# A hybrid attention layer on one core: masked score sums and their maximum in one VectorE operation, and rotary operands laid out for two heads at a time

## The chip, the cores and the metric

The kernel runs on one core of one Trainium2 chip. The metric is the device time in microseconds (us) of one execution. Before the change it is 898.43 us, the median of three runs (897.34 to 899.4). TensorE (PE) multiplies matrices into PSUM, VectorE (DVE) and ScalarE (ACT) do the element work, GpSimd (POOL) issues some of the transfers, and SyncE (SP) issues the rest.

## The reference, cut to what matters

One decoder layer, 512 tokens, width 2048, all in float32. The normed input is projected once and split; eight MLA heads and eight forgetting (FoX) heads run side by side, each output is gated, and one output projection and a norm follow.

```python
h = _rms_norm(x, g_pre); proj = h @ w_in                    # 2048 -> latents, gates, fq, fk, fv, f_logit
# FoX head: c is the running sum of the log forget gates
c = cumsum(log_sigmoid(f_logit + b_forget))
logits = (q @ k.T) * HEAD_DIM**-0.5 + c[q_pos] - c[k_pos]
# MLA head: 128 plain columns, 64 rotary columns; the rotary key is shared by all heads
logits = (q_nope @ k_nope.T + rope(q_rope) @ rope(k_rope).T) * QK**-0.5
# both: causal mask, softmax over keys, in blocks of 128 queries
p = softmax(where(key <= query, logits, -inf)); o = p @ v
out = x + _rms_norm(concat(o_mla * silu(gate_mla), o_fox * silu(gate_fox)) @ w_out, g_post)
```

The term c[q_pos] is the same for a whole row of logits, and a softmax over the row does not depend on it.

## The kernel before, in words

**Products.** Every large product is made of three passes (`mm3`, L149 to L151): each operand is split into a high part and a low part, rounded by ScalarE (`act.copy`) and subtracted by VectorE, and high times high, high times low and low times high are summed in PSUM. Weight chunks of 512 KB come in on SP's queue (`load`), ScalarE writes `whi` (L276), VectorE writes `wlo` (L279). Several projections are done with seven block products in place of eight, which gives VectorE additional block sums (L266, L946).

**Order of the work.** The program is straight-line code. Small work (scores, transposes of probabilities, values, splits) is put into a list `todo`, and `pump` takes entries from it between the matmuls of a projection; `drain` empties it. A planner then orders each engine's instructions by its own costs and the program's priorities; a few instructions are pinned with `in_order`. Big tiles (4 KB per partition) come from a pool of 28 slots.

**Stages.** 0 to 40 us: first columns of the input projection. 40 to 235 us: FoX gates, values, first queries and keys. 235 to 435 us: four FoX pairs of heads; the scores of one pair are pumped into the next pair's projections. 435 to 600 us: latents and MLA gates. 600 to 750 us: four MLA pairs. From 718 us on: output projection.

**A block of scores** (`Head.scores`, from L616) serves one head and 128 queries `b`; it holds n = 128(b+1) keys in one PSUM bank of the three of `att_bank`. For b = 0 the operands are whole float32 blocks; for the others two or three passes per kind of column. Then, before the change:

- FoX: `ccol` holds c per query. VectorE adds c[q] - c[k] in place in PSUM, once for the columns below the diagonal block (L636) and once for the diagonal block, whose key row has the mask added (L639). MLA: the mask is added to the diagonal block in place (L630).
- VectorE takes the negated row maximum (L643); for MLA ScalarE scales it by the query's norm (L649, `qcol`).
- ScalarE takes the exponential from PSUM into the tile `p` in SBUF and sums the row (L650); VectorE divides by the sum (L651, L652).

`forget_cols` (L784) turns c by four transposes on PE into `ccol`. `load_keys` (L790) broadcasts one head's c to 128 partitions by one transfer of 256 KB; `forget_keys` (L795) negates it and adds the mask to its four diagonal blocks.

**Rotary operands.** `rotary_key` (L1103) turns the shared key, 64 rows, and leaves in `kr` its high part in rows 0 to 63 and its low part in rows 64 to 127. It is the last step of the rotary tables (list `rot`, L1193) and runs at 164 to 171 us. Per MLA pair, `rotate` makes two products `a` and `b` of the two heads' 128 rotary rows; four additions of 64 rows (L1514) write each head's turned query twice into a tile `rq`; `rq` is split (L138, L139) for the blocks from 128 on, and its first 128 columns are copied (L126). Both passes multiply by the same `kr`.

Of the kernel before, what the change touches and what calls it, by code (L numbers as in the profile page):

```python
# [43 lines left out]
L4 = KVR // 2  # L44
KL = L4 + ROPE
NSLOT = 28
DEEP, EXTRA = 6, 3
# [18 lines left out]
def tile_hybrid_layer(  # L66
# [42 lines left out]
    def att_bank(name):  # L109
        return bank("at", name, 3)  # L110
# [60 lines left out]
    gains = cst.tile([NK, P], F32, name="gains")  # L171
    gains2 = cst.tile([P, P], F32, name="gains2")
    pool.memset(gains2, 0.0)
    xk = [None] * NK
# [20 lines left out]
    make_identity(nc, ident)  # L195
    mask = cst.tile([P, P], F32, name="mask")
    make_causal_mask(nc, mask, mask_val=NEG)
# [410 lines left out]
    class Head:  # L608
# [7 lines left out]
        def scores(self, b):  # L616
            n = (b + 1) * P
            nn = n
            s = att_bank(f"s{self.name}{b}")
            qs = slice(b * P, n)  # L620
            pairs = []
            if b == 0:
                pairs, nn = self.whole, P
            else:
                for kind, (qh, ql), (kh, kl) in zip(("nope", "rope"), self.q, self.k):
                    pairs += [(qh, kh), (qh, kl), (ql, kh)] if kind == "nope" else [(qh, kh), (ql, kh)]
            for i, (a, c) in enumerate(pairs):
                pe.matmul(s[:, :nn], a[:, qs], c[:, :nn], start=(i == 0), stop=(i == len(pairs) - 1))  # L628
            if self.fox is None:
                dve.tensor_tensor(out=s[:, qs], in0=s[:, qs], in1=mask, op=ALU.add)  # L630
            else:
                nk, nkm, h = self.fox
                cq = ccol[:, b, h : h + 1]
                if b:
                    m = b * P
                    dve.scalar_tensor_tensor(  # L636
                        out=s[:, :m], in0=s[:, :m], scalar=cq, in1=nk[:, :m], op0=ALU.add, op1=ALU.add
                    )
                dve.scalar_tensor_tensor(  # L639
                    out=s[:, qs], in0=s[:, qs], scalar=cq, in1=nkm[:, qs], op0=ALU.add, op1=ALU.add  # L640
                )
            st = pp.tile([P, 3], F32, tag="st", name=f"st{self.name}{b}", bufs=4)
            dve.tensor_reduce(out=st[:, 0:1], in_=s[:, :n], op=ALU.max, axis=AX.X, negate=True)  # L643
            p = pp.tile([P, n], F32, tag=f"p{b}", name=f"p{self.name}{b}")
            unit = 1.0
            if self.fox is None:

                unit = qcol[:, b : b + 1]
                act.mul(st[:, 0:1], st[:, 0:1], unit)  # L649
            act.activation(p, s[:, :n], AF.Exp, bias=st[:, 0:1], scale=unit, accum_out=st[:, 1:2])  # L650
# [61 lines left out]
    pool.memset(rf, 0.0)  # L712
    ccol = cst.tile([P, NT, NH], F32, name="ccol")
    c_dram = dr.tile([NH, S], F32, name="c_dram")
# [17 lines left out]
    def forget_sums(r):  # L732
# [28 lines left out]
        def scan():  # L761
# [17 lines left out]
            two(ln, ln, d, ALU.add),  # L779
            both(z, z, 0.0, ln, ALU.min, ALU.subtract),  # L780
            scan,
        ]

    def forget_cols():  # L784
        pt = att_bank("ccol")
        for t in range(NT):
            pe.transpose(pt[:, t * P : (t + 1) * P], rf[:, t * P : (t + 1) * P], ident)
        dve.tensor_copy(ccol, pt.rearrange("p (t c) -> p t c", t=NT)[:, :, R])

    def load_keys(h):  # L790
        both = slot(f"nk{h}")
        nc.sync.dma_start(both[:, 0, :], c_dram[h : h + 1, :].to_broadcast([P, S]))
        return both, h

    def forget_keys(both, h):  # L795

        nk, nkm = both[:, 0, :], both[:, 1, :]
        in_order(dve.tensor_scalar(out=nk, in0=nk, scalar1=-1.0, scalar2=None, op0=ALU.mult))
        for b in range(NT):
            c = slice(b * P, (b + 1) * P)  # L800
            dve.tensor_tensor(out=nkm[:, c], in0=nk[:, c], in1=mask, op=ALU.add)
        return nk, nkm, h

# [72 lines left out]

    HALF = S // 2
    oper = {}
# [224 lines left out]
    def rotary_key():  # L1103

        a, b = rotate(rf, ROPE, 1.0, "k")
        dve.tensor_tensor(out=a[:ROPE, :], in0=a[:ROPE, :], in1=b[:ROPE, :], op=ALU.add)
        act.copy(kr[:ROPE, :], a[:ROPE, :])
        dve.tensor_tensor(out=kr[ROPE:, :], in0=a[:ROPE, :], in1=kr[:ROPE, :].bitcast(F32), op=ALU.subtract)

    kr = tb.tile([P, S], F32R, name="kr")  # L1110

# [80 lines left out]
    rot = rotary_tables()  # L1192
    rot.append(rotary_key)  # L1193
    wait(1)
# [33 lines left out]
    k = fox_k(0, wholes)  # L1228
    forget_cols()
    drain()  # L1230
# [17 lines left out]
    v_out(c21, 1, 0)  # L1248
    keys = [load_keys(6 + i) for i in range(2)]
    seconds.clear()  # L1250
# [6 lines left out]
    for p in range(4):  # L1257
        if p:
            q, wholes = fox_q(p)
            drain()  # L1260
            keys = [load_keys(2 * (3 - p) + i) for i in range(2)]
            vt = load_v(3 - p, v_slot(3 - p))
# [9 lines left out]
        if p == 2:  # L1272
            nc.sync.dma_start(gains2[0:6, :], g_q.rearrange("o (k p) -> (o k) p", p=P))
            nc.sync.dma_start(gains2[6:10, :], g_kv.rearrange("o (k p) -> (o k) p", p=P))
            make_gcol(gains2, NK, 10)
        vs = values_of(f"fv{3 - p}")
# [41 lines left out]
    lat_diag = {}  # L1318
    qcol = cst.tile([P, NT], F32, name="qcol")

    def latent_stats(j):
# [15 lines left out]
        if j == 0:  # L1337
            dve.scalar_tensor_tensor(out=qcol, in0=y, scalar=SC_M, in1=rcol, op0=ALU.mult, op1=ALU.mult)
            return
# [161 lines left out]
    for p in range(4):  # L1501
# [6 lines left out]
        qw = [[whole_block(wholes, i, qb[i])] for i in range(2)]  # L1508
        a, b = rotate(qb[2], P, 1.0, f"q{p}")
        for i in range(2):  # L1510
            r = tmp(f"rq{p}{i}")
            src = slice(ROPE * i, ROPE * (i + 1))
            for half in range(2):
                dve.tensor_tensor(  # L1514
                    out=r[ROPE * half : ROPE * (half + 1), :], in0=a[src, :], in1=b[src, :], op=ALU.add
                )
# [16 lines left out]
        for i in c["kv"]:  # L1533
            hi, lo = chunk(i)
            for j in range(chunks[i][3]):
# [13 lines left out]
                paced(hi)  # L1549
        k = [[split(kb[i], f"mk{p}{i}"), (kr, None)] for i in range(2)]  # L1550
        kw = [[whole_block(wholes, 2 + i, kb[i]), kr.bitcast(F32)[:, :P]] for i in range(2)]
        drain()
# [238 lines left out]
```

## Time and profile before

| what | value |
|---|---|
| median of three runs | 898.43 us (897.34 to 899.4) |
| the profiled execution | 897.76 us, its span 896.0 us, 1.76 us around it |
| granted TensorE clock, mean | 0.997 |
| PE busy | 883.9 us (99%) |
| VectorE busy | 678.7 us (76%) |
| ScalarE busy | 453.8 us (51%) |
| DMA | 218.26 MB, mean 244 GB/s |

The profile is of one execution. A busy share is the time in which an engine has at least one instruction in flight; matmuls overlap, so the mean duration of a matmul is longer than the distance from one to the next. An "idle before" belongs to the engine just ahead of an instruction, and the name behind it is what ended it.

### The profile page before, as it was taken

What the parts mean: (1) busy time and instruction counts of PE and PEld (TensorE: products, weight loads), DVE (VectorE), ACT (ScalarE), POOL (GpSimd) and SP (SyncE); (2) the same over time, 40 slices, a digit from 0 to 9 for tenths busy, and PEclk for the clock granted to TensorE, in tenths of its full rate; (3) what the DMA queues carried; (4) which work ended last, traced back from release to release, by engine and by line L of the source; (5) the groups of instructions that cost most, each with busy time, mean ns of one, the idle gap of its engine ahead of it and who ended that gap; (6) DMA issues with size and microseconds to landing.
All of it is one profiled execution on the core that took longest, in us unless ns stands there. A gap on an engine that the chain in (4) does not pass through costs nothing.

```text
span 896.0 us, 12851 instructions
## 1 busy us (share of the span) xinstructions
PE 883.9 (99%) x4598; PEld 755.2 (84%) x4598; DVE 678.7 (76%) x1123; ACT 453.8 (51%) x837; POOL 65.7 (7%) x86
## 2 busy tenths in 40 slices
PE   9999999999999999999999999999999999999996
PEld 8988887888888888888998998788888888888885
DVE  4579995648766838577588898967877995988785
ACT  6944443334344323335445565535555676646383
POOL 1010110011211101000000000000000000000021
PEclk9999999999999999999999999999999999999998
DMA  9798799789899999996899984799762137799878
GB/s 294 235 265 250 215 322 298 233 237 305 242 278 274 245 235 254 243 267 154 275 395 393 342 297 138 159 235 233 190 147 91 51 118 219 239 325 312 269 217 250
DMA packets 125659, 218.26 MB, mean 244 GB/s; under 512 B 16378, under 2 KB 54036, under 8 KB 124572
## 3 DMA queue, kind: packets, MB, share of 16 engines
q1 hardware_dynamic: 113484, 179.47, 61.2%
q0 software_dynamic: 11376, 37.75, 20.7%
q8 instruction: 36, 0.59, 0.3%
q10 hardware_dynamic: 736, 0.22, 0.1%
q14 instruction: 27, 0.22, 0.1%
HBM read 202.72 MB, written 65.03 MB: 299 GB/s over the span
## 4 chain that ended last, share of the span: by engine, by line
PE 85%; DVE 8%; DMA 3%; ACT 2%; issue 1%; SPq 0%; DVEq 0%; ACTq 0%
PE fk L149 3%; PE fk L151 3%; PE fq L149 3%; PE fk L150 3%; PE fq L151 3%; PE fq L150 3%; PE in L585 3%; PE sm L628 2%; DVE wlo L279 2%; PE fg L149 2%; PE fg L150 2%; PE fg L151 2%; PE oa L149 2%; PE oa L151 2%; PE oa L150 2%; PE mq L149 2%
## 5 line engine op out<-in xcount | busy, mean ns | idle before, releaser
L279 DVE TENSOR_TENSOR wlo<-raw,whi 128x1024 fp32r<-128x1024 f32 (+3 forms) x217 | 256.7, 1187 | 128.2 <-ACT whi L276 125.6
L276 ACT CAST whi<-raw 128x1024 fp32r<-128x1024 f32 (+3 forms) x217 | 221.1, 1023 | 259.3 <-PE fk L150 34.1
L149 PE MATMUL fk<-h,whi 128*128 128x512 f32 x128 | 52.5, 410 | 0.0
L149 PE MATMUL fq<-h,whi 128*128 128x512 f32 x128 | 50.8, 397 | 0.0
L149 PE MATMUL fg<-h,whi 128*128 128x512 f32 x128 | 50.3, 393 | 0.0
L151 PE MATMUL fk<-h,wlo 128*128 128x512 f32 x128 | 50.2, 393 | 0.0
L150 PE MATMUL fk<-h,whi 128*128 128x512 f32 x128 | 50.1, 391 | 0.0
L151 PE MATMUL fq<-h,wlo 128*128 128x512 f32 x128 | 50.0, 390 | 0.0
L150 PE MATMUL fq<-h,whi 128*128 128x512 f32 x128 | 49.9, 390 | 0.0
L151 PE MATMUL fg<-h,wlo 128*128 128x512 f32 x128 | 49.9, 390 | 0.0
L150 PE MATMUL fg<-h,whi 128*128 128x512 f32 x128 | 49.9, 390 | 0.0
L266 DVE TENSOR_TENSOR raw<-raw,second 128x1024 f32<-128x1024 f32 x32 | 39.0, 1218 | 0.3 <-DMA second<-in_w_out_dram 0.3
L650 ACT ACTIVATE pf<-sf,stf 128x128 f32<-128x128 f32 (+3 forms) x32 | 16.7, 524 | 33.4 <-DVE stf L643 33.4
L585 PE MATMUL in<-whi,h 128*128 128x328 f32 x128 | 29.9, 321 | 0.3 <-ACT h L143 0.3
L149 PE MATMUL mq<-ln,whi 128*128 128x512 f32 x72 | 28.8, 400 | 0.0
L151 PEld LDWEIGHTS fk<-h,wlo 128*128 128x128 f32 x128 | 24.0, 188 | 5.4
L151 PEld LDWEIGHTS fq<-h,wlo 128*128 128x128 f32 x128 | 24.0, 188 | 5.3
L151 PEld LDWEIGHTS fg<-h,wlo 128*128 128x128 f32 x128 | 24.0, 188 | 5.1
L150 PE MATMUL mq<-ln,whi 128*128 128x512 f32 x72 | 28.3, 393 | 0.0
L151 PE MATMUL mq<-ln,wlo 128*128 128x512 f32 x72 | 28.2, 391 | 0.0
L149 PEld LDWEIGHTS fg<-h,whi 128*128 128x128 f32 x128 | 24.1, 188 | 4.7
L150 PEld LDWEIGHTS fg<-h,whi 128*128 128x128 f32 x128 | 24.1, 188 | 4.7
(566 smaller groups left out, 2467.1 us busy)
## 6 DMA issues: line engine op xcount, KB each, us to landing
raw<-in_w_in_dram SPq DMA_DIRECT2D x96, 512.0 KB
raw<-in_w_out_dram SPq DMA_DIRECT2D x32, 512.0 KB
second<-in_w_in_dram SPq DMA_DIRECT2D x24, 512.0 KB
bmg<-awaymg SPq DMA_DIRECT2D x20, 256.0 KB
awaymg<-rmg POOLq DMA_DIRECT2D x8, 512.0 KB, 7.5
raw<-t6v SPq DMA_DIRECT2D x8, 512.0 KB
t7o<-in_w_out_dram SPq DMA_DIRECT2D x4, 1024.0 KB
t7o<-in_w_out_dram POOLq DMA_DIRECT2D x4, 1024.0 KB, 10.2
```

Of the source, the lines that this page charges most:

```text
L149: pe.matmul(o, ah, bh, start=first, stop=False, **kw)
L150: pe.matmul(o, ah, bl, start=False, stop=False, **kw)
L151: pe.matmul(o, al, bh, start=False, stop=last, **kw)
L266: tc.keep_in_program_order(dve.tensor_tensor(out=raw, in0=raw, in1=second, op=ALU.add))
L276: cast = act.copy(hi[:, :m], raw[:, :m])
L279: dve.tensor_tensor(out=lo[:, :m], in0=raw[:, :m], in1=hi[:, :m].bitcast(F32), op=ALU.subtract)
L585: pe.matmul(banks[t][:, :n], a[k][:, tss[t]], b[:, j, :], start=k == 0 and m == 0, stop=k == NK - 1 and m == 2,)
L628: pe.matmul(s[:, :nn], a[:, qs], c[:, :nn], start=(i == 0), stop=(i == len(pairs) - 1))
L650: act.activation(p, s[:, :n], AF.Exp, bias=st[:, 0:1], scale=unit, accum_out=st[:, 1:2])
```

## The change: what it does

**Scores.** One VectorE operation, `tensor_tensor_reduce`, takes the scores in PSUM and a row tile in SBUF over all n columns, adds them, multiplies by -1 and writes the result to `p` in SBUF; the same operation gives the row's minimum, which is the negated maximum of the sums. The exponential then runs in place on `p` with scale -1 (FoX) or -`qcol` (MLA, `nqcol`). c[q] is not added any more, so `ccol`, its four transposes and its copy are gone.

**Rows.** For MLA the row is a tile of zeros, 384 wide, with the mask behind it, and its last n columns are taken. For FoX the scan sums the negated logs, so that c arrives negated, and four masked blocks are put beside unmasked ones: this takes a second broadcast of 256 columns (128 KB) per head into the other half of the head's slot, and the block for b = 0 goes to a free part of `wholes`.

**Rotary queries.** `a + b` is formed once over 128 rows for both heads. Per head one tile `r` has the high part in the head's own 64 rows and the low part in the other 64. Both heads' `r` share one slot.

**Rotary key.** Two tiles (one slot) hold the key's high part twice and its low part twice; the two passes multiply the same `r` by each. `warm` keeps the unsplit first 128 columns twice. `rotary_key` moves from the end of `rot` to `todo` before the last gate projection `fox_g(3)`.

**Small tiles.** `gains2` (128 rows, cleared by POOL) goes; the later gains are loaded into `gains` (16 rows) and transposed from there.

```diff
+    rows_mask = cst.tile([P, S], F32, name="mask")
+    pool.memset(rows_mask[:, : S - P], 0.0)
+    mask = rows_mask[:, S - P :]
...
-                    pairs += [(qh, kh), (qh, kl), (ql, kh)] if kind == "nope" else [(qh, kh), (ql, kh)]
+                    pairs += [(qh, kh), (qh, kl)] + ([(ql, kh)] if kind == "nope" else [])
...
+            st = pp.tile([P, 3], F32, tag="st", name=f"st{self.name}{b}", bufs=4)
+            p = pp.tile([P, n], F32, tag=f"p{b}", name=f"p{self.name}{b}")
+            to, src, row = p, s[:, :n], rows_mask[:, S - n :]
+            if self.fox is not None:
+                row = self.fox[b]
...
+            dve.tensor_tensor_reduce(
+                out=to, in0=src, in1=row, scale=-1.0, scalar=-NEG, op0=ALU.add, op1=ALU.min,
+                accum_out=st[:, 0:1],
+            )
+            unit = -1.0
             if self.fox is None:
-                dve.tensor_tensor(out=s[:, qs], in0=s[:, qs], in1=mask, op=ALU.add)
-            else:
-                nk, nkm, h = self.fox
-                cq = ccol[:, b, h : h + 1]
...
-            dve.tensor_reduce(out=st[:, 0:1], in_=s[:, :n], op=ALU.max, axis=AX.X, negate=True)
...
+                unit = nqcol[:, b : b + 1]
+                act.mul(st[:, 0:1], st[:, 0:1], qcol[:, b : b + 1])
+            act.activation(p, p, AF.Exp, bias=st[:, 0:1], scale=unit, accum_out=st[:, 1:2])
...
+            number(z, z, -1.0, ALU.mult),
             scan,
...
-    def forget_cols():
-        pt = att_bank("ccol")
-        for t in range(NT):
-            pe.transpose(pt[:, t * P : (t + 1) * P], rf[:, t * P : (t + 1) * P], ident)
-        dve.tensor_copy(ccol, pt.rearrange("p (t c) -> p t c", t=NT)[:, :, R])
...
+        nc.sync.dma_start(both[:, 1, :HALF], c_dram[h : h + 1, :HALF].to_broadcast([P, HALF]))
+        return both, wholes[:, 1, h % 2 * P : (h % 2 + 1) * P]
...
-        in_order(dve.tensor_scalar(out=nk, in0=nk, scalar1=-1.0, scalar2=None, op0=ALU.mult))
...
+        for n, (to, src) in enumerate(
+            ((first, 0), (less[:, 3, :], 1), (less[:, 2, :], 2), (full[:, 3, :], 3))
+        ):
+            masked = dve.tensor_tensor(out=to, in0=full[:, src, :], in1=mask, op=ALU.add)
+            if n == 0:
+                in_order(masked)
+        return first, less[:, 0::3, :], both[:, 1, : 3 * P], both[:, 0, :]
...
-        act.copy(kr[:ROPE, :], a[:ROPE, :])
-        dve.tensor_tensor(out=kr[ROPE:, :], in0=a[:ROPE, :], in1=kr[:ROPE, :].bitcast(F32), op=ALU.subtract)
...
+        act.copy(krh[:ROPE, :], k)
+        act.copy(krw[:ROPE, :], k[:, :P])
+        hi = krh[:ROPE, :].bitcast(F32)
+        for half in range(2):
+            dve.tensor_tensor(
+                out=krl[half * ROPE : (half + 1) * ROPE, :], in0=k, in1=hi, op=ALU.subtract
+            )
+        dve.tensor_copy(krh[ROPE:, :], hi)
+        dve.tensor_copy(krw[ROPE:, :], k[:, :P])
...
-    rot.append(rotary_key)
...
+    todo.append(rotary_key)
     fox_g(3, two_of(proj_bank, "fg3"))
...
+        dve.tensor_tensor(out=a, in0=a, in1=b, op=ALU.add)
+        turned = slot(f"rq{p}", F32R)
         for i in range(2):
-            r = tmp(f"rq{p}{i}")
-            src = slice(ROPE * i, ROPE * (i + 1))
-            for half in range(2):
-                dve.tensor_tensor(
-                    out=r[ROPE * half : ROPE * (half + 1), :], in0=a[src, :], in1=b[src, :], op=ALU.add
-                )
-            q[i].append(split(r, f"rq{p}{i}", first=P))
-            qw[i].append(whole_block(wholes, 4 + i, r))
+            r = turned[:, i, :]
+            hi, lo = (slice(ROPE * h, ROPE * (h + 1)) for h in (i, 1 - i))
+            split_into(r[hi, :], r[lo, :], a[hi, :])
+            q[i].append((r, None))
+            qw[i].append(r.bitcast(F32))
```

More of the change, by code (lines that the diff above doesn't have):

```diff
@@ L45 @@
 KL = L4 + ROPE
+HALF = S // 2
 NSLOT = 28
@@ new lines, in scores @@
+            p = pp.tile([P, n], F32, tag=f"p{b}", name=f"p{self.name}{b}")
+            to, src, row = p, s[:, :n], rows_mask[:, S - n :]
+            if self.fox is not None:
+                row = self.fox[b]
+                if len(row.shape) == 3:
+                    to, src = (a.rearrange("p (b c) -> p b c", c=P) for a in (to, src))
+            dve.tensor_tensor_reduce(
+                out=to, in0=src, in1=row, scale=-1.0, scalar=-NEG, op0=ALU.add, op1=ALU.min,
+                accum_out=st[:, 0:1],
+            )
@@ L780, in forget_sums, with load_keys, forget_keys @@
             both(z, z, 0.0, ln, ALU.min, ALU.subtract),
+            number(z, z, -1.0, ALU.mult),
             scan,
         ]
-    def forget_cols():
-        pt = att_bank("ccol")
-        for t in range(NT):
-            pe.transpose(pt[:, t * P : (t + 1) * P], rf[:, t * P : (t + 1) * P], ident)
-        dve.tensor_copy(ccol, pt.rearrange("p (t c) -> p t c", t=NT)[:, :, R])
-    def load_keys(h):
+    def load_keys(h, wholes):
         both = slot(f"nk{h}")
         nc.sync.dma_start(both[:, 0, :], c_dram[h : h + 1, :].to_broadcast([P, S]))
[L793 to L802, printed above, removed]
+        nc.sync.dma_start(both[:, 1, :HALF], c_dram[h : h + 1, :HALF].to_broadcast([P, HALF]))
+        return both, wholes[:, 1, h % 2 * P : (h % 2 + 1) * P]
+    def forget_keys(both, first):
+        full, less = (both[:, i, :].rearrange("p (b c) -> p b c", b=NT) for i in range(2))
+        for n, (to, src) in enumerate(
[5 more added lines that the diff above has]
+        return first, less[:, 0::3, :], both[:, 1, : 3 * P], both[:, 0, :]
     cosT = tb.tile([P, S], F32, name="cosT")
@@ L874, in rotate @@
         return a, b
-    HALF = S // 2
     oper = {}
@@ L1248, in tile_hybrid_layer @@
     v_out(c21, 1, 0)
-    keys = [load_keys(6 + i) for i in range(2)]
+    keys = [load_keys(6 + i, wholes) for i in range(2)]
     seconds.clear()
@@ L1260, in tile_hybrid_layer @@
             drain()
-            keys = [load_keys(2 * (3 - p) + i) for i in range(2)]
+            keys = [load_keys(2 * (3 - p) + i, wholes) for i in range(2)]
             vt = load_v(3 - p, v_slot(3 - p))
@@ L1318, in tile_hybrid_layer @@
     lat_diag = {}
-    qcol = cst.tile([P, NT], F32, name="qcol")
+    qcol, nqcol = (cst.tile([P, NT], F32, name=n) for n in ("qcol", "nqcol"))
     def latent_stats(j):
@@ L1337, in latent_stats @@
         if j == 0:
-            dve.scalar_tensor_tensor(out=qcol, in0=y, scalar=SC_M, in1=rcol, op0=ALU.mult, op1=ALU.mult)
+            for to, scale in ((qcol, SC_M), (nqcol, -SC_M)):
+                dve.scalar_tensor_tensor(out=to, in0=y, scalar=scale, in1=rcol, op0=ALU.mult, op1=ALU.mult)
             return
```

36 lines of the change are left out of this document (10 added, 26 removed).

## The prediction, made before the changed kernel ran

> **What bounds the kernel now.** I read the page first, then the table of stretches, then what PE waited for, then the chain of waits. The page:
>
> ```profile
> PE 883.9 (99%) x4598; PEld 755.2 (84%) x4598; DVE 678.7 (76%) x1123; ACT 453.8 (51%) x837; POOL 65.7 (7%) x86
> ```
>
> PE is busy 883.9 of the span's 896.0 us. Whatever is taken from VectorE or ScalarE can return at most PE's idle time, 896.0 - 883.9 = 12.1 us. The table of stretches (length, then busy us of each engine) tells where that idle time is:
>
> ```profile
> 0.00:22.40 22.40, 20.86 (x141) 20.12 (x142) 10.16 (x16) 15.49 (x45) 2.39 (x13) 1.00 0.96 294
> 200.00:300.00 100.00, 99.89 (x464) 82.41 (x463) 72.83 (x141) 39.93 (x76) 16.07 (x18) 1.00 0.95 271
> 400.00:500.00 100.00, 99.91 (x639) 90.95 (x638) 75.67 (x101) 50.75 (x75) 3.76 (x6) 1.00 0.89 306
> 600.00:700.00 100.00, 99.60 (x566) 86.92 (x565) 81.79 (x177) 56.37 (x146) 3.62 (x4) 1.00 0.64 159
> 700.00:800.00 100.00, 99.41 (x502) 83.79 (x501) 85.30 (x138) 62.73 (x117) 0.00 (x0) 1.00 0.58 189
> 873.00:896.00 23.00, 15.55 (x66) 11.93 (x64) 13.87 (x30) 8.76 (x18) 3.52 (x4) 0.90 0.88 249
> ```
>
> The start (22.40 - 20.86 = 1.5 us) and the end (23.00 - 15.55 = 7.5 us) hold nine of the twelve, and the change edits nothing of the end. In the stretches of the scores PE lacks 0.1, 0.1, 0.4 and 0.6 us. Of PE's waits by the releaser these touch edited work or its neighbours:
>
> ```profile
> PE oa L149 <- ACT mw L126: 0.6, 1, 0.6
> PE sm L628 <- ACT pm L650: 0.4, 1, 0.4
> ```
>
> So PE's own work is the bound, and the question is which of its instructions and which of its few waits go, and whether the new order brings a wait.
>
> **The change part by part: PE's own work.** `forget_cols` goes. Its four transposes stand as one piece of the chain:
>
> ```profile
> 196.11 0.44 PE ccol L787 x4
> ```
>
> That is 0.44 us of PE time with nothing beside it: -0.44. The score passes keep their number and width: for b from 128 on, two rotary passes of the same weights' size before and after (high and low query by one key before, one query by high and low key after), and at b = 0 one whole block each. The later transpose of gains stays one transpose, of 16 rows and not 128; I count nothing for it.
>
> **The scores' VectorE work.** Groups by line, busy us and mean ns of one; L702 is the same kind of operation at 512 columns, and the ScalarE row is the only reading of an accumulator in the trace:
>
> ```profile
> L643 DVE TENSOR_REDUCE stf<-sf 128x1 f32<-128x128 f32 (+3 forms) x32 | 15.6, 487 | 0.6
> L643 DVE TENSOR_REDUCE stm<-sm 128x1 f32<-128x128 f32 (+3 forms) x32 | 15.2, 484 | 0.4
> L636 DVE SCALAR_TENSOR_TENSOR sf<-sf,ccol,nk 128x128 f32<-128x128 f32 (+2 forms) x24 | 11.7, 486 | 2.3 <-PE sf L628 2.3
> L639 DVE SCALAR_TENSOR_TENSOR sf<-sf,ccol,nk 128x128 f32<-128x128 f32 x32 | 11.2, 352 | 0.4
> L630 DVE TENSOR_TENSOR sm<-sm,mask 128x128 f32<-128x128 f32 x32 | 9.0, 293 | 3.6 <-PE sm L628 3.2
> L702 DVE SCALAR_TENSOR_TENSOR ghf<-fg,rrow 128x512 f32<-128x512 f32 x8 | 5.2, 683 | 0.1
> L650 ACT ACTIVATION_READ_ACCUMULATOR pf<-sf,stf 128x1 f32 x32 | 6.2, 193 | 0.0
> ```
>
> Removed: 15.6 + 15.2 + 11.7 + 11.2 + 9.0 = 62.7 us. Added: 64 operations that no row shows. They read one PSUM and one SBUF stream and write one SBUF stream. Lower bound: the reductions alone, 15.6 + 15.2 = 30.8 us. Upper bound: an addition of the full width by L636 and L702, 3 x 0.486 + 0.683 = 2.14 us per head, 16 heads 34.3 us, and a separate reading of the accumulator at ScalarE's 0.193, 64 x 0.193 = 12.4 us: 46.7 us. I take the upper, whose streams are those of the new operation: VectorE has 16 us less to do, between 16 and 32.
>
> [...]
>
> The exponential reads `p` in SBUF and not PSUM any more. The nearest rows are the copies of one width, from SBUF (`rq`) and from PSUM (`mq`):
>
> ```profile
> L126 ACT COPY mw<-rq 128x128 f32<-128x128 f32 x8 | 2.4, 294 | 0.0
> L126 ACT COPY mw<-mq 128x128 f32<-128x128 f32 x8 | 2.1, 264 | 0.0
> ```
>
> That is 64 x 0.03 = 1.9 us more on ScalarE, in stretches where it is busy 40 to 63 of 100 us: nothing on the path.
>
> **What this frees.** The PSUM bank of a block is released by VectorE's operation, and no longer by ScalarE's exponential behind it. PE's wait of 0.40 us is of that kind, in PE's and ScalarE's timeline:
>
> ```profile
> 621.09 0.67 ACT L650 ACTIVATE pm<-sm,stm,qcol 128x384 f32<-128x384 f32 x1
> 621.90 0.62 PE L628 MATMUL sm<-mk,mq 128*128 128x256 f32 x3 [0.40 <-ACT pm L650]
> ```
>
> The third bank comes free at 621.8, at the end of an exponential that began at 621.09; with the change it is free before that begins. I take the whole wait off: -0.40, between 0 and -0.40. Next late could be the transposes of `p`, which only come sooner.
>
> **Rotary queries, keys' rows.**
>
> ```profile
> L1514 DVE TENSOR_TENSOR rq<-raq,rbq 64x512 f32<-64x512 f32 x16 | 11.0, 686 | 0.4
> L139 DVE TENSOR_TENSOR rq<-rq,rq 128x384 fp32r<-128x384 f32 x8 | 4.4, 556 | 0.1
> L798 DVE TENSOR_SCALAR nk<-nk 128x512 f32<-128x512 f32 x8 | 3.4, 421 | 3.4 <-DMA nk<-c_dram 3.4
> L138 ACT CAST rq<-rq 128x384 fp32r<-128x384 f32 x8 | 4.1, 511 | 11.1 <-DVE rq L1514 11.1
> ```
>
> Per pair four additions and two subtractions (4 x 0.686 + 2 x 0.556 = 3.9 us) become one addition and two subtractions of 512 columns (3 x 0.686 = 2.1 us): 7 us less on VectorE over four pairs, and 3.4 us less for the negations of L798. ScalarE loses two casts and two copies (2 x 0.511 + 2 x 0.294 = 1.6 us) for two casts of 64 rows (2 x 0.62, the key's cast below): 0.4 us less per pair. The wait of 0.6 us at `oa` (718 us) is for ScalarE's last copy out of the fourth pair's key bank; a shorter queue ahead of it may shorten it, but the planner's order decides. I take half: -0.30, between 0 and -0.59.
>
> **The moved key.** Its steps in the trace, and the rows of the two stretches into which it moves:
>
> ```profile
> L865 DVE SCALAR_TENSOR_TENSOR rak<-rf,cosT 64x512 f32<-64x512 f32 x1 | 0.7, 673 | 0.0
> L870 DVE SCALAR_TENSOR_TENSOR rbk<-rf,sinT 32x512 f32<-32x512 f32 x2 | 1.4, 681 | 0.0
> L1107 ACT CAST kr<-rak 64x512 fp32r<-64x512 f32 x1 | 0.6, 620 | 1.9 <-DVE rak L1106 1.9
> L1108 DVE TENSOR_TENSOR kr<-rak,kr 64x512 fp32r<-64x512 f32 x1 | 0.7, 685 | 0.0
> ```
>
> ```profile
> 395.00:405.00 10.00, 10.00 (x48) 8.38 (x47) 8.50 (x24) 4.26 (x10) 0.00 (x0) 1.00 1.00 323
> 405.00:415.00 10.00, 10.00 (x48) 8.33 (x47) 6.58 (x19) 2.64 (x7) 0.86 (x1) 1.00 0.89 199
> ```
>
> After: 0.67 + 1.36 + 0.68 (the sum) + 2 x 0.685 + two copies (0.42 by L798, at most, each) = 4.5 to 4.9 us on VectorE, 0.9 us on ScalarE. In the 20 us before 415 VectorE is idle for 20 - 8.50 - 6.58 = 4.9 us, and the pair's scores give back 2 x (62.7 - 46.7) / 16 = 2 us on average. It fits if it runs there as its inputs, old by then, allow; I count 0. The price where it doesn't is a rival below. What it leaves, 164 to 171 us, is not on PE's path.
>
> **Transfers.** Each pair's `load_keys` issues two more broadcasts of 128 KB on SP's queue, ahead of the values and of the weights:
>
> ```profile
> 363.71 0.83 SPq L792 DMA_DIRECT2D nk<-c_dram  x2
> 364.63 1.43 SPq L1137 DMA_DIRECT2D fv<-v_away  x1
> 366.40 0.38 SPq L256 DMA_DIRECT2D raw<-in_w_in_dram  x1
> ```
>
> ```profile
> SPq L256 <- DVE wlo L279: 202.1, 75, 12.8
> ```
>
> Two issues of 0.4 us and 256 KB at the mean 244 GB/s, 1.1 us, put the next chunk back by up to 1.9 us. The last row (SP's waits: in total, times, longest) says that loads stand ready and wait for VectorE to free a buffer, 202 us in 75 times, so the cover is about 2.7 us a time. Cost 0; without the cover 4 x 1.9 = 7.6 us.
>
> **The sum.** The profiled execution took 897.76 us: its span 896.0 and 1.76 around it. 897.76 - 0.44 - 0.40 - 0.30 = 896.6. It stands 0.67 below the median shown, so I put the same on: 897.3 us.
>
> **The rivals.**
> - *Faster, by waits too short to be listed.* Matmuls overlap, so a delay below their latency shows as a longer matmul. In the groups by shape the first pass `fk` L149 has a mean of 410 ns, L150 391, and L149 of `mk` 420:
>
> ```profile
> L149 PE MATMUL fk<-h,whi 128*128 128x512 f32 x128 | 52.5, 410 | 0.0
> L150 PE MATMUL fk<-h,whi 128*128 128x512 f32 x128 | 50.1, 391 | 0.0
> L149 PE MATMUL mk<-ln,whi 128*128 128x512 f32 x32 | 13.4, 420 | 0.0
> ```
>
>  That is 128 x 19 + 32 x 29 = 3.4 us in passes that stand behind scores and transposes. Most of it may be the turn from one kind of pass to another, which stays. If half is delay by VectorE, and the `oa` wait goes whole: 897.3 - 1.7 - 0.3 = 895.3.
> - *Nothing but the transposes.* The relief is real and PE meets other waits of the same size, as the planner orders anew: 897.76 - 0.44 + 0.67 = 898.0, with new waits to 899.5. For it: all the edited work lies beside a PE that is 99% busy.
> - *Slower: the key in front of the gates.* `rotary_key` is emitted by the `drain` just ahead of `fox_g(3)`'s gates. If VectorE runs it there, 4.7 us stand before the first reading of the gate banks:
>
> ```profile
> 415.38 0.69 DVE L702 SCALAR_TENSOR_TENSOR ghf<-fg,rrow 128x512 f32<-128x512 f32 x1
> 416.66 0.36 PE L149 MATMUL gl<-h,whi 128*128 128x256 f32 x1
> ```
>
>  The next product on PE starts 0.6 us after that reading ends (416.07), in a bank of the same four. 4.7 - 0.6 = 4.1 us of waiting, 901.4 us. It decides from the point where more than 0.6 us of the turn is undone at 415.4. Against it: VectorE's 4.9 us of gaps just before.
> - *The one operation isn't cheap.* If its rate were half of an addition's, 68.6 + 12.4 = 81 us against 62.7, 1.1 us more per head, less the 0.9 us per head of the rotary work in MLA. The MLA stretches leave VectorE about 15 of 100 us: still 898 to 899, and counted with the second rival.
>
> **How the numbers follow.** The forecast has 0.45, faster 0.20, nothing but the transposes (with the slow operation) 0.20, slower 0.15. From no change a measurement of this kernel can tell about 0.2%, 1.8 us: below 896.6 is faster, above 900.2 slower. The forecast's own range, 896.3 to 898.1 by the bounds 0 to -0.40 and 0 to -0.59 and the spread of runs, lies a little under 896.6: 0.10 of its 0.45 is faster. With nearly all of the faster rival that is 0.28; slower gets 0.15 and 0.02 of the third; 0.55 remain. The range goes from the faster rival, 895.3, to near the slower one, 900.9.
>
> **What would show it.** Right: no `ccol` group; one VectorE group of 64 in the scores, 0.4 to 0.9 us each, VectorE 25 us less busy; no PE wait on the exponential; the key's turn finished before the last gate reading; PE still at 99%. Wrong: PE waits at 415 to 421 us, on weights at 230 to 400 us, or a new wait in the four MLA pairs.

## The result: slower by about 1%

The changed kernel takes 908.75 us, the median of its runs (906.4 to 912.77); the kernel before, in the same comparison, takes 898.91 us. The ratio is 1.0112, with a 95% interval of 1.0064 to 1.016: about 10 us slower. The forecast was 897.3 us, its range 895.2 to 900.9. The profiled execution is the fastest of the four, 906.4 us with a span of 904.6; so the trace explains 8.6 us of span (904.6 - 896.0), and what the other executions lost beyond that is in no trace. The mean granted clock of each execution is on record: 0.994 in the two shorter ones, 0.992 and 0.991 in the two longer (910.77 and 912.77 us), so these spent more time at a lowered clock.

The page of the kernel after, its span and its busy times:

```profile
span 904.6 us, 12808 instructions
...
PE 889.1 (98%) x4594; PEld 758.3 (84%) x4594; DVE 647.8 (72%) x1083; ACT 456.8 (50%) x830; POOL 66.0 (7%) x86
```

VectorE lost 30.9 us of work (678.7 to 647.8), more than forecast, and PE has four instructions fewer, the transposes. Still PE is busy 5 us longer, and its idle time rose from 12.1 to 15.5 us. PE's waits after, by the releaser (in total, times, longest), tell of the second:

```profile
PE pvf L152 <- DVE fv3l L140: 4.1, 1, 4.1
...
PE pvf L151 <- DVE plf L140: 0.4, 1, 0.4
...
PE mv L150 <- DVE rbq L864: 0.4, 1, 0.4
PE pvm L151 <- DVE plm L140: 0.4, 1, 0.4
```

None of the four stands in the list of the kernel before; `sm` on the exponential and `oa` on ScalarE's copy, which stood there, are gone. One wait is ten times the others. PE's timeline after, at that place:

```profile
259.72 0.40 PE L151 MATMUL pvf<-plf,fv3h 128*128 128x512 f32 x1
264.24 0.80 PE L152 MATMUL pvf<-phf,fv3l 128*128 128x512 f32 x1 [4.13 <-DVE fv3l L140]
264.84 0.63 PE L150 MATMUL fk<-h,whi 128*128 128x512 f32 x1
265.26 0.63 PE L151 MATMUL fk<-h,whi 128*128 128x512 f32 x1
```

PE waits for the low part of the values. Then its matmuls take 0.63 us in place of 0.40: the columns of the table of stretches (length, busy us of each engine, granted clock, DMA share, GB/s) show why.

```profile
200.00:300.00 100.00, 95.75 (x432) 78.67 (x431) 61.98 (x119) 37.72 (x70) 16.06 (x18) 0.97 0.94 267
...
264.30:270.00 5.70, 5.70 (x15) 4.43 (x16) 3.48 (x9) 1.32 (x2) 0.00 (x0) 0.50 1.00 228
270.00:300.00 30.00, 30.00 (x147) 25.01 (x146) 14.11 (x29) 10.54 (x23) 5.52 (x6) 1.00 0.93 227
```

Behind the wait the granted clock is 0.50 for 5.7 us. That is the part that shows as busy PE. What held `fv3l` up is in VectorE's timeline after:

```profile
257.68 0.69 DVE L140 TENSOR_TENSOR plf<-ptf,phf 128x512 fp32r<-128x512 f32 x1
262.70 0.49 DVE L793 TENSOR_TENSOR nk<-nk,mask 128x128 f32<-128x128 f32 x2 [4.34 <-DMA nk<-c_dram]
263.11 0.16 DVE L648 RECIPROCAL stf<-stf 128x1 f32<-128x1 f32 x1
263.19 0.27 DVE L793 TENSOR_TENSOR nk<-nk,mask 128x128 f32<-128x128 f32 x1
263.38 0.48 DVE L649 TENSOR_SCALAR pf<-pf,stf 128x512 f32<-128x512 f32 x1
263.77 1.09 DVE L140 TENSOR_TENSOR fv3l<-fv,fv3h 128x256 fp32r<-128x256 f32 x3
```

L793 is the mask's addition to the keys' row of the next pair of heads. It has come up on VectorE at 258.4, waits 4.34 us there for the broadcast of that row, and everything behind it waits too, the division of a finished block and the value split among it. Before the change the additions for the same pair (L801) ran here, in VectorE's timeline of the kernel before:

```profile
286.26 0.42 DVE L798 TENSOR_SCALAR nk<-nk 128x512 f32<-128x512 f32 x1
286.71 0.90 DVE L801 TENSOR_TENSOR nk<-nk,mask 128x128 f32<-128x128 f32 x4
```

They ran 24 us later, behind the negation, when the transfer was long done.

**A ledger of where the time went.** Each matmul of the kernel before can be put beside the same matmul (same tiles, same turn) of another kernel's trace; the difference of their starts is what the other has lost until there. Medians of these differences in us, over the 10 us of the kernel before that begin at the time named (the kernels come below):

```
at (before)    120    180    230    280    400    600    620    660    740    860
after         0.85  -0.01  -0.48   6.51   7.40   7.38   7.10   8.59   8.14   8.67
all held      0.63  -0.22  -0.71  -0.77  -0.56  -0.61  -1.26   0.12  -0.29   0.93
rotary only  -0.18  -0.18  -0.22  -0.27  -0.30  -0.39   0.13   0.11  -0.56  -0.46
FoX new       0.03  -0.84  -1.33  -1.44  -1.20  -1.20  -0.22  -0.27  -0.89  -0.62
MLA new       0.67   0.66   0.65   0.63   0.66   0.58  -0.07   0.97   0.56   1.93
```

Up to 180 us the rows differ by up to 1.7 us, which is put down to what changes from one execution to the next; each row is a single trace. From 180 to 230 us the removed transposes give 0.47 us. Between 250 and 280 us the changed kernel loses 7.0 us: 4.13 by the wait, 2.8 by the clock. Some 0.9 us go at 310 to 340 us. The wait on `plf` is among them: ahead of that split, additions for the following pair of heads wait 2.24 and 2.55 us on VectorE for their rows, as at 258 us; with all additions held (below) neither these waits nor that on `plf` are there. In the MLA pairs 1.2 us net are lost, and `oa` gives back 0.6 at 720. VectorE waits for rows six times in the changed kernel, 14.6 us in all; a listed wait of PE stands behind three of the six.

### The profile page after: what moved, and what is told of

Its sections match the earlier page's. It is cut to its first block, busy times and chain, and to the rows that moved or that the text cites. A ratio compares the mean times of both kernels' runs of the same rounds, so it can differ in the third digit from the quotient of the medians.

```text
span 904.6 us, 12808 instructions
## 1 busy us (share of the span) xinstructions
PE 889.1 (98%) x4594; PEld 758.3 (84%) x4594; DVE 647.8 (72%) x1083; ACT 456.8 (50%) x830; POOL 66.0 (7%) x86
## 4 chain that ended last, share of the span: by engine, by line
PE 54%; DMA 5%; DVE 3%; ACT 1%; issue 1%; SPq 0%; DVEq 0%; ACTq 0%
PE sm L629 2%; PE oa L150 2%; PE oa L152 2%; PE oa L151 2%; DMA raw<-in_w_ukv_dram 1%; DMA t4o<-in_w_out_dram 1%; PE od L151 1%; PE od L152 1%; PE fk L150 1%; PE fk L152 1%; PE fk L151 1%; PE oc L150 1%; PE od L150 1%; PE oc L151 1%; PE oc L152 1%; DMA raw<-t7o 1%
## 5 line engine op out<-in xcount | busy, mean ns | idle before, releaser
L150 PE MATMUL fk<-h,whi 128*128 128x512 f32 x128 | 53.5, 418 | 0.0
L151 PE MATMUL fk<-h,whi 128*128 128x512 f32 x128 | 51.0, 399 | 0.0
L647 ACT ACTIVATE pf<-pf,stf 128x128 f32<-128x128 f32 (+3 forms) x32 | 18.0, 564 | 62.4 <-DVE stf L638 62.4
L150 PEld LDWEIGHTS fk<-h,whi 128*128 128x128 f32 x128 | 24.7, 193 | 4.5
L151 PEld LDWEIGHTS fk<-h,whi 128*128 128x128 f32 x128 | 24.7, 193 | 4.0
```

The costliest lines, as they stand in the source:

```text
L150: pe.matmul(o, ah, bh, start=first, stop=False, **kw)
L151: pe.matmul(o, ah, bl, start=False, stop=False, **kw)
L647: act.activation(p, p, AF.Exp, bias=st[:, 0:1], scale=unit, accum_out=st[:, 1:2])
```

## The experiments

**Theories.** A: the pin (`in_order`) sat on the negation, and the four additions had to follow it because they read what it wrote. With the negation gone only the addition that writes `first` is pinned; the planner takes the other three ahead on VectorE's queue, where they wait for the transfer, and nothing behind them runs meanwhile (for 4.34 us above). B: the second broadcast per head delays the transfers (128 KB more each on SP's queue), and the additions are only where that shows. C, from the forecast's rivals: the key's turn or the new operation costs it.

**All four additions held in order.**

```diff
             masked = dve.tensor_tensor(out=to, in0=full[:, src, :], in1=mask, op=ALU.add)
-            if n == 0:
-                in_order(masked)
+            in_order(masked)
```

> The changed kernel with all four mask additions of each head's key row pinned in program order, not only the first. Theory A (the additions lost the order that the pinned negation gave them, float ahead on VectorE's queue, and wait there for a transfer while the value split stands behind them): the wait of 4.1 us at 260 us and the halved clock behind it are gone, granted clock 0.997 again, 897.5 to 899 us, 7 to 9 us under the changed kernel. Rival B (the second broadcast makes the key rows late, wherever the additions stand): a wait for the key rows remains, at 285 us and later, 903 us or more. Rival C (the new operation, the moved key and the rest cost the time and the wait is only where it shows): 903 us or more without a listed wait.

Measured: 898.72 us, ratio 1.0006 (0.9994 to 1.0019). The whole loss, as far as can be told, is gone with one edit of order. PE's waits in this kernel:

```profile
PE od L151 <- DVE wlo L280: 0.9, 2, 0.6
PE gcm L151 <- DVE wlo L280: 0.8, 2, 0.6
PE mv L150 <- DVE rbq L863: 0.4, 1, 0.4
PE pvm L151 <- DVE plm L140: 0.4, 1, 0.4
```

No wait on `fv3l`, and the stretch of 200 to 300 us is back at 99.87 us of PE. A holds, C falls: this kernel has the new operation and the moved key. The kernel isn't faster than the one before either.

**One broadcast, the additions free.** The second broadcast is replaced by a copy on VectorE.

```diff
-        nc.sync.dma_start(both[:, 1, :HALF], c_dram[h : h + 1, :HALF].to_broadcast([P, HALF]))
...
+        dve.tensor_copy(less[:, :2, :], full[:, :2, :])
```

> The changed kernel without the second broadcast per head: VectorE copies the two unmasked blocks (256 columns) instead, and the pins stay as in the changed kernel. Theory A: the additions still float and still wait; a listed PE wait of 2 us or more on VectorE's value split stays, 902 to 909 us. Rival B: the wait goes, 897 to 900 us.

Measured: 910.14 us, ratio 1.0133 (1.0115 to 1.0152). PE's wait, and VectorE's timeline:

```profile
PE pvf L152 <- DVE fv3l L140: 5.9, 1, 5.9
```

```profile
266.54 0.29 DVE L789 COPY nk<-nk 128x256 f32<-128x256 f32 x1 [6.15 <-DMA nk<-c_dram]
```

With a third less to transfer (256 KB per head in place of 384) the wait is longer, not shorter; now it is the copy that stands ahead. B falls as the cause.

**The kernel before, with only its pin taken off.**

```diff
-        in_order(dve.tensor_scalar(out=nk, in0=nk, scalar1=-1.0, scalar2=None, op0=ALU.mult))
+        dve.tensor_scalar(out=nk, in0=nk, scalar1=-1.0, scalar2=None, op0=ALU.mult)
```

> The kernel before with nothing changed but the pin on the negation of the key row taken off; one broadcast, old operations. Theory A: the negation floats ahead on VectorE to just before the value split of the second pair and waits there for its transfer; if that lands as in the changed kernel (8 us behind its issue) PE waits 1 to 4 us there, and longer than before by 1 to 8 us, 900 to 906 us. Rivals B and C: as before, 898 to 899 us.

Measured: 904.01 us, ratio 1.0069 (1.0053 to 1.0084). More than half of the loss comes without any other part of the change, in the same place:

```profile
PE pvf L151 <- DVE fv3l L139: 3.8, 1, 3.8
```

```profile
265.89 0.61 DVE L798 TENSOR_SCALAR nk<-nk 128x512 f32<-128x512 f32 x1 [4.30 <-DMA nk<-c_dram]
266.42 0.47 DVE L652 TENSOR_SCALAR pf<-pf,stf 128x512 f32<-128x512 f32 x1
266.81 1.08 DVE L139 TENSOR_TENSOR fv3l<-fv,fv3h 128x256 fp32r<-128x256 f32 x3
```

Now the negation itself is what waits. With the kernel held in order this shows the cause from both sides: take the order away from the old kernel and it loses, give it back to the new one and it loses nothing that can be told.

**The kernel before, with a second broadcast.**

```diff
+        nc.sync.dma_start(both[:, 1, : S // 2], c_dram[h : h + 1, : S // 2].to_broadcast([P, S // 2]))
```

> The kernel before with the second broadcast of 128 KB per head added (it lands in the half that the masked blocks overwrite). Theory A: as before within 2 us, 897 to 901 us. Rival B: 903 us or more, with a PE wait at 235 to 400 us.

Measured: 898.97 us, ratio 1.0017 (1.0001 to 1.0033), and no PE wait between 235 and 400 us. Its `sm` wait on the exponential is 1.1 us in this trace and 0.4 before; by the ledger that is where it differs. The second broadcast costs 0.17% by the middle of the interval, 1.5 us, and between 0.1 and 3 us by its ends; 0.7 us of it is this wait in the trace; the forecast's price without cover was 7.6 us.

**The keys fetched earlier, the additions free.** Both broadcasts are issued ahead of the pair's query projection.

```diff
+            rows = [fetch_keys(2 * (3 - p) + i) for i in range(2)]
             q, wholes = fox_q(p)
             drain()
-            keys = [load_keys(2 * (3 - p) + i, wholes) for i in range(2)]
+            keys = [load_keys(2 * (3 - p) + i, wholes, rows[i]) for i in range(2)]
...
```

> The changed kernel, its mask additions free as they are, with both broadcasts of a pair's keys issued ahead of that pair's query projection and not behind it. If the loss is the wait of the early additions for that transfer (theory), the transfer is done when they come up: no PE wait on fv3l, no half clock, 898 to 900 us. If it lies in the additions' place on VectorE alone, the time stays at 905 to 909.

Measured: 909.4 us, ratio 1.0127 (1.0099 to 1.0155). The expectation that the wait would go was wrong. VectorE's timeline, and the issue on SP's queue:

```profile
238.82 0.16 DVE L648 RECIPROCAL stf<-stf 128x1 f32<-128x1 f32 x1
246.47 0.29 DVE L796 TENSOR_TENSOR nk<-nk,mask 128x128 f32<-128x128 f32 x1 [7.49 <-DMA nk<-c_dram]
```

```profile
242.69 0.32 SPq L783 DMA_DIRECT2D nk<-c_dram  x1
```

The additions moved with the load. One comes up on VectorE at 239.0, 3.7 us before its transfer is even issued, and waits 7.49 us. It looks as if the planner puts a free addition where it expects the input, and the real transfer comes later than that; the times that the planner reckons with are not on record. What the two kernels show is that an earlier load doesn't mend the early place in VectorE's queue, on which nothing ran in those 7.49 us, and a pin does. PE's waits here are spread (2.3 us on `fv3h`, 1.7 on `stf` at the transposes, 0.8 at `sf`).

**Value splits made long on purpose.** To price a wait by its length, the first subtraction of `fv3l` was done 8 or 14 times in the kernel with all additions held (`again` is 7 or 13 for that pair of heads).

```diff
             split_into(hi[:, cols], lo[:, cols], parts[t], pin=pin)
+            for _ in range(again if t == 0 else 0):
+                in_order(
+                    dve.tensor_tensor(
+                        out=lo[:, cols], in0=parts[t], in1=hi[:, cols].bitcast(F32), op=ALU.subtract
+                    )
+                )
...
```

> The kernel with all four mask additions held in order, in which the first subtraction of fv3l (0.36 us, pair of heads 6 and 7) is done eight times in place of once, each held in order, so that the third pass of pvf at 259.7 us waits about 7 x 0.36 - 0.3 = 2.2 us; the result doesn't change. It measures what a wait of a given length costs there. If a wait costs its own length and no more: 898.7 + 2.2 = 900.9 us and a granted clock of 1.00 behind it. If the half clock seen behind the waits of 3.8 to 5.9 us follows any wait of some us: 2.2 + about 3.6 more, 904.5 us, and a stretch at 0.5 to 0.8. If it needs a length between 2.2 and 3.8 us: 900.9, too, and the run with the long wait tells the two apart.

> The same with fourteen subtractions in place of one: the wait is about 13 x 0.36 - 0.3 = 4.4 us, and nothing in it waits for a transfer. If the wait is all that the changed kernel lost: 898.7 + 4.4 = 903.1 us and a clock of 1.00. If the clock falls behind any long wait of PE, whatever it is for: 903.1 + about 3.6 = 906.7 us, with some 5 us at a clock near 0.5. If the half clock belongs to the late transfer and not to the idle PE, it doesn't come here.

Measured: 899.23 us (1.0009, 1.0 to 1.0017) and 898.38 us (1.0003, 0.9992 to 1.0014). Both miss every theory named: there is no wait at all. PE in the second kernel, where the third pass comes 7.7 us after the second:

```profile
261.80 0.39 PE L151 MATMUL pvf<-plf,fv3h 128*128 128x512 f32 x1
...
269.50 0.50 PE L152 MATMUL pvf<-phf,fv3l 128*128 128x512 f32 x1
```

In between PE runs mostly matmuls of `fk` (PE is busy 20.00 of the 20 us from 255 to 275). This work on VectorE is absorbed: other products stand in the gap, as they would if the planner counts its length. So VectorE's additional work (653.6 us in all against 647.8) cost nothing that can be told, where 4.3 us of waiting for a transfer cost 7. The two kernels don't price a wait; the clock is read from the others, below.

**The parts alone.** Three kernels divide the rest of the change: the kernel before with the rotary part alone ("rotary only"); the held kernel with the MLA scores as before ("FoX new"); the kernel before with the rotary part and the new operation in MLA ("MLA new"). The core of their edits, in this order (the second against the held kernel, the third against rotary only):

```diff
+    todo.append(rotary_key)
     fox_g(3, two_of(proj_bank, "fg3"))
```

```diff
+            if self.fox is None:
+                dve.tensor_tensor(out=s[:, qs], in0=s[:, qs], in1=mask, op=ALU.add)
+                dve.tensor_reduce(out=st[:, 0:1], in_=s[:, :n], op=ALU.max, axis=AX.X, negate=True)
```

```diff
+            if self.fox is None:
+                dve.tensor_tensor_reduce(
+                    out=p, in0=s[:, :n], in1=rows_mask[:, S - n :], scale=-1.0, scalar=-NEG,
...
```

> The kernel before with the rotary part alone: one sum for two heads, the key doubled in two tiles, its turn moved ahead of the last gate product; the scores, the mask and the keys' rows as before. As predicted, it is worth 0 to -0.6 us (the wait of oa), so 897.4 to 898 against 898.0 of the kernel before. If the new waits of the held kernel in the MLA pairs (mv on rbq 0.4 us, pvm on plm 0.4) come from this part, they are here too, and the time is 0 to +1 us: 898 to 899. With the key's turn in front of the gates (rival): +4.1 us.

> The kernel with all four mask additions held in order, in which the MLA heads keep their old addition, maximum and exponential from PSUM; the FoX scores, the keys' rows and the rotary part are the new ones. If the new waits in the MLA pairs (mv on rbq 0.4 us, pvm on plm 0.4) come from the new score operation there, by the new order it gives VectorE, they go and the time is 0.5 to 0.8 us below the held kernel: 897.6 to 898.2. If they come from the planner's order whatever the scores are, others of that size stand in the list and the time stays at 898.5 +- 0.5.

> The kernel before with the rotary part and with the new score operation in the MLA heads only; FoX scores, ccol and the keys' rows as before. If the waits in the MLA pairs come from the new operation there, mv or pvm waits of about 0.4 us each are here, and the time is 0.5 to 0.8 us above the kernel with the rotary part alone (897.8): 898.3 to 898.6. If not, the exponential's release of the bank is the only thing that changes: the wait sm on pm (0.9 us in that kernel) goes, and the time is 897.0 to 897.8.

Measured: rotary only 897.84 us (0.9992, 0.9983 to 1.0); FoX new 898.01 (0.9993, 0.9982 to 1.0004); MLA new 898.97 (1.0002, 0.999 to 1.0014). None beats the kernel before by what can be told. The waits, of rotary only, FoX new and MLA new in turn:

```profile
PE sm L628 <- ACT pm L650: 0.9, 1, 0.9
```

```profile
PE sm L629 <- ACT pm L636: 1.4, 1, 1.4
```

```profile
PE mv L149 <- DVE rbq L874: 0.4, 1, 0.4
```

Where the MLA exponential reads PSUM, PE waits for it (`sm`, 0.9 and 1.4 us), and `mv` doesn't wait. Where the new operation is used in MLA, `sm` doesn't wait on the exponential, and `mv` waits for the rotary products. In the ledger MLA new gains 0.65 between 600 and 620 us (0.58 to -0.07) and has lost 1.04 by 660. In these traces one wait takes the other's place.

**Rotary products ahead of the query splits.** An attempt to take that wait off in the held kernel.

```diff
+        a, b = rotate(qb[2], P, 1.0, f"q{p}")
         q = [[split(qb[i], f"mq{p}{i}", first=P)] for i in range(2)]
...
-        a, b = rotate(qb[2], P, 1.0, f"q{p}")
```

> The kernel with all four mask additions held in order, in which the products of rotate are emitted ahead of the splits of the two query banks and not behind them. If the wait mv on rbq (0.4 us, at 635.7) is due to the place of the products behind the splits, it goes, and the time falls by up to 0.4 us, to 898.3, below the resolution of a median but to be seen in the list of waits. If the planner sets that order by its own costs, nothing changes; if the splits come too late, a wait of mk or sm takes its place.

Measured: 899.72 us, ratio 1.002 (1.0005 to 1.0034), and the wait became 0.6, with a second one beside it: `mv` on ScalarE's copy `mw`, 0.6. The new order is no better. The profiled execution (span 902.1) also lost 3.0 us between 130 and 145 us, ahead of anything that this edit touches in the program. Its trace shows what was lost there: PE waits 0.96 and 0.76 us for the two halves of one weight chunk (at `vg`), and the clock is at half for 3.4 us behind them. How much of the median that is stays open.

## Why the prediction was wrong, point by point

**The step that failed** is "Rotary queries, keys' rows", in its words "3.4 us less for the negations of L798". It counted the negation as work. It was also the only pinned instruction of the keys' rows, and by its in-place result it held the four additions L801. The diff shows the pin going to one of four additions, and the front part names pins; the prediction never asked what the other three would now be free to do, and what stands behind them on VectorE. Its own row of L798 had the warning, "3.4 <-DMA nk<-c_dram 3.4": the negation waits for the transfer even when held. The kernel before without its pin (1.0069) and the changed one with four pins (1.0006) show it from both sides. In the ledger the former loses 5.6 us there and the changed kernel 7.0: waits of 3.8 and 4.1 us, and half clock for 3.4 and 6.8 us behind them.

**The slower rival was the wrong one.** The key's turn in front of the gates did not happen. VectorE's timeline after has the key's last step and the first gate reading at:

```profile
409.13 0.22 DVE L1112 COPY warm<-rak 64x128 f32<-64x128 f32 x1
...
422.78 1.38 DVE L699 SCALAR_TENSOR_TENSOR ghf<-fg,rrow 128x512 f32<-128x512 f32 x2
```

The turn was done 13 us ahead, in VectorE's gaps, at the cost of 0 that was counted. That its price (4.1 us) is near the wait found is chance: other place, other mechanism. A wait of PE "on weights at 230 to 400 us" was named among what would make the prediction wrong; the wait came in that stretch, but on a value split behind a row of keys.

**PE's own work** was right: four instructions fewer, -0.44 forecast, -0.47 in the ledger.

**The new operation** was mis-sized on VectorE, and it didn't matter. Its groups after (line, operation, tiles, count; busy us, mean ns; idle before):

```profile
L638 DVE CUSTOM_DVE_ANT_0 pm<-sm,mask 128x128 f32<-128x128 f32 (+3 forms) x32 | 15.0, 485 | 3.4 <-PE sm L629 3.4
...
L638 DVE CUSTOM_DVE_ANT_0 pf<-sf,nk 128x384 f32<-128x384 f32 (+1 forms) x16 | 9.9, 619 | 6.6 <-PE sf L629 6.6
...
L638 DVE CUSTOM_DVE_ANT_1 pf<-sf,nk 128x256 f32<-128x256 f32 x8 | 3.4, 421 | 3.8 <-PE sf L629 3.8
...
L638 DVE DVE_READ_ACCUMULATOR2_ANT stm<- 128x1 f32 x32 | 2.7, 83 | 0.0
L638 DVE DVE_READ_ACCUMULATOR2_ANT stf<- 128x1 f32 x32 | 2.6, 82 | 0.0
...
L638 DVE CUSTOM_DVE_ANT_0 pf<-sf,fw 128x128 f32<-128x128 f32 x8 | 2.3, 285 | 0.3
```

Together 15.0 + 9.9 + 3.4 + 2.7 + 2.6 + 2.3 = 35.9 us, between the bounds 30.8 and 46.7 and nearer the lower. The main part, 30.6 us, costs what the maximum alone cost (30.8): the addition, the scaling and the write to SBUF add nothing that can be told. The reading of the accumulator is 0.083 us, and not ScalarE's 0.193. Each of the 64 operations has such a reading in a row of its own (32 and 32). Before the change no run had shown one on VectorE; the 12.4 us that the upper bound counts for it were the author's estimate, and the runs showed 2.7 + 2.6 = 5.3 us. That the reading is so short is what the sum lacked. So VectorE fell by 30.9 us in all and not by 25.

**The exponential from SBUF** costs ScalarE 564 - 524 = 40 ns more in FoX and 654 - 618 = 36 in MLA (the smaller numbers are the means of L650 before), 32 of each, 2.4 us and not 1.9. The rows after:

```profile
L647 ACT ACTIVATE pm<-pm,stm,nqcol 128x128 f32<-128x128 f32 (+3 forms) x32 | 20.9, 654 | 1.0
...
L647 ACT ACTIVATE pf<-pf,stf 128x128 f32<-128x128 f32 (+3 forms) x32 | 18.0, 564 | 62.4 <-DVE stf L638 62.4
```

**The two small waits** went as forecast, and more: `sm` gives 0.65 in the held kernel, and `oa` 0.6, the whole of it (forecast 0.40 and 0.30). What the forecast left out is that in the MLA pairs `pvm` and `mv` take their place at 0.7 us each in the ledger (-1.26 at 620, -0.54 at 630, 0.12 at 660). That is its rival "nothing but the transposes", for all that was left when the order was mended: 898.0 to 899.5 forecast, 898.72 measured. The held kernel also loses 1.2 us between 740 and 860 us, part of it in waits of `od` on split weights (0.9 us, 0.3 before); MLA new loses 1.4 there, the other rows of the ledger 0.1 to 0.5. These are single traces, and why is open.

**The faster rival**, half of the long first passes of `fk` as hidden delay by VectorE, is refuted. In the groups by shape of the held kernel, with 30.9 us less on VectorE:

```profile
L150 PE MATMUL fk<-h,whi 128*128 128x512 f32 x128 | 52.5, 410 | 0.0
```

The same 410 ns. A short delay does show as a longer matmul: in the kernel before `vp` at 215.95 us starts 0.50 us behind the matmul ahead of it, where its neighbours start 0.23 apart, and takes 0.50 us in place of 0.39, with no listed wait. But VectorE's load is not what makes these passes of `fk` long; that it is the turn from one kind of pass to another, as the forecast allowed, no run tests.

**Transfers** were counted 0. The kernel before with a second broadcast is slower by 0.01 to 0.33%, with no wait of PE behind a row or a weight that the kernel before doesn't have: near enough to 0, and far from 7.6 us.

## What to carry to other kernels

A pinned instruction holds, beside itself, everything that depends on it: before one is removed, list what reads its result and give the pin to each of these. Where an instruction that waits holds up all that stands behind it, as it did on VectorE here (4.34 and 7.49 us), ask of every instruction that a change sets free which transfer it waits for, and what on the critical engine stands behind it; a delay of known length was hidden here, a wait for a transfer was not. Work taken from an engine that isn't the bound (31 us of VectorE's) bought nothing.

## What the runs showed of the hardware

A wait of PE cost more than its length here: 4.13 us of waiting in the kernel after went with a loss of 7.0 us in the ledger. In its trace the granted clock is either full or half (length, then busy us of each engine, granted clock, DMA share, GB/s):

```profile
0.00:263.17 263.17, 258.93 (x1244) 219.99 (x1244) 183.41 (x278) 126.78 (x233) 31.36 (x47) 1.00 0.89 267
263.17:270.00 6.83, 5.76 (x15) 4.49 (x16) 4.61 (x14) 1.32 (x2) 0.00 (x0) 0.50 0.98 239
270.00:901.47 631.47, 624.37 (x3337) 533.84 (x3335) 459.81 (x793) 328.69 (x595) 34.66 (x39) 1.00 0.78 233
901.47:904.60 3.13, 0.00 (x0) 0.00 (x0) 0.00 (x0) 0.00 (x0) 0.00 (x0) 0.50 0.36 127
```

In this kernel and four others it fell to 0.50 during waits of PE or behind them and came back after about 3.4 us or twice that. From the mean clock of the microseconds at both ends (a mean c is a share 2(1 - c) at half), in the kernel after:

```profile
263.00:264.00 1.00, 0.00 (x0) 0.00 (x0) 1.00 (x5) 0.00 (x0) 0.00 (x0) 0.59 0.87 315
...
270.00:271.00 1.00, 1.00 (x7) 0.91 (x6) 0.00 (x0) 0.00 (x0) 0.00 (x0) 1.00 1.04 279
```

That is 0.82 us of the first and the whole of the next six: 6.8 us, of which PE ran matmuls for 5.7; at half speed these lose 2.8, the rest of the 7.0 us in the ledger. In the kernel with one broadcast (wait 5.9 us) it is 6.8 us, too, by the same reading (0.30 + 6 + 0.52). In the one with the keys fetched earlier, where PE waited 0.8, 0.9 and 2.3 us within 8 us, it is 0.62 + 2 + 0.80 = 3.4 us. The kernel before without its pin has 3.4 us behind a wait of 3.8 us, and the one with the rotary products first 3.4 us behind waits of 0.96 and 0.76 us.

The moments at which the clock of the kernel after changes, 263.17, 270.00 and 901.47 us, are 6.83 and 631.47 us apart: 2 and 185 times 3.4133 us. Here are stretches of that length, in the kernel after, in the one with the rotary products first, and in the one with 14 subtractions, where PE waits 0.81 and 0.77 us at `vg`:

```profile
259.76:263.17 3.41, 0.35 (x2) 0.00 (x0) 0.47 (x3) 0.50 (x2) 2.01 (x2) 1.00 0.64 224
263.17:266.58 3.41, 2.34 (x6) 1.86 (x7) 2.48 (x10) 0.00 (x0) 0.00 (x0) 0.50 0.88 238
266.58:270.00 3.42, 3.42 (x11) 2.64 (x10) 2.13 (x5) 1.32 (x2) 0.00 (x0) 0.50 1.08 240
```

```profile
138.05:141.46 3.41, 1.69 (x6) 0.86 (x5) 2.17 (x3) 2.95 (x3) 0.00 (x0) 1.00 0.93 324
141.46:144.87 3.41, 3.41 (x9) 2.63 (x8) 2.19 (x3) 0.00 (x0) 0.00 (x0) 0.50 0.88 252
```

```profile
138.91:142.32 3.41, 1.84 (x7) 1.31 (x8) 2.63 (x3) 2.65 (x3) 0.00 (x0) 1.00 0.87 297
142.32:145.73 3.41, 3.41 (x17) 2.83 (x16) 3.07 (x4) 1.06 (x1) 0.00 (x0) 1.00 0.93 297
```

PE was idle for 3.06, 1.72 and 1.57 us in the first stretch of each; half clock followed in the first two and not in the third. In the second, no single wait is longer than 0.96 us. What sets the clock, and whether there is a bound between 1.57 and 1.72 us, these rows don't tell. The 4.13 us of the kernel after lie as 3.06 us ahead of the clock's fall and 1.07 us behind it, and the clock is at half for 6.8 us. In the kernel before without its pin all of the 3.8 us lie ahead of the fall, 2.73 of them in the last 3.41 us, and half clock for 3.4 us follows.
